# Top-2 gate dispatch: the first group's loads and stores cut at other rows

## The chip, the cores and the metric

The kernel runs on one core of a Trainium2 chip. The metric is the device time of one execution in microseconds. Before the change it is 239.73 us, the median of three runs (239.54 to 239.82). The profile shows the engines that take part: VectorE (DVE) for the products, ScalarE (ACT) for the sigmoids and a few small things, SyncE (SP) as the issuer of most DMAs, and the core's 16 DMA engines, which carry everything between HBM and the on-chip memory.

## The reference

16 x 1024 tokens have 512 numbers each and 8 router logits. For each token the two largest softmax probabilities are normalized to a sum of 1, and the token's numbers are written out twice, once times each of the two weights, the smaller first.

```python
def reference(x, router_logits, k):          # x [16, 1024, 512], logits [16, 1024, 8], k = 2
    logits_max = np.max(router_logits, axis=-1, keepdims=True)
    probs = np.exp(router_logits - logits_max)
    probs = probs / np.sum(probs, axis=-1, keepdims=True)
    topk_indices = np.argsort(probs, axis=-1)[..., -k:]
    topk_probs = np.take_along_axis(probs, topk_indices, axis=-1)
    topk_probs = topk_probs / np.sum(topk_probs, axis=-1, keepdims=True)
    x_expanded = x[:, :, np.newaxis, :].repeat(k, axis=2)
    return (x_expanded * topk_probs[..., np.newaxis]).astype(np.float32)
```

Input and output together are 101.2 MB: 33.6 MB of x, 0.5 MB of logits, and 67.1 MB of output.

## The kernel before, in words

**Rows.** The 16,384 tokens are spread over 128 partitions. A "row" below is one token in each partition, so 128 tokens, and there are 128 rows: 65 in group 0 and 63 in group 1 (`GROUPS`). A row is 2,048 B for each partition in x and 4,096 B in the output, where each token stands twice. In HBM the rows that one partition loads or stores in one DMA lie next to each other, so such a DMA of n rows is 128 runs, one for each partition, eight for each of the 16 DMA engines.

**Buffers.** `xs` holds 65 rows of x. `osp` holds 18 output rows; at the start it also lends its place to the logits and the scratch of the top-2 search. `WA` holds the two weights of every row. Output is built either in `osp` or in `xs` itself, over rows whose x has been used up (a "store in xs" of 16 rows takes the place of 32 rows of x). `STORES` lists for each group, store by store: first row, number of rows, buffer, and place in it.

**Loads.** `LOADS` gives the DMAs of x by rows, group 0 as 6, 28 and 31, group 1 as 4, 28 and 31. `BASE` is the first row of `xs` for each group. All are issued by SyncE (line 139), except the 4-row load of group 1, which ScalarE issues behind a small copy that waits until the last store but one of group 0 has landed (lines 123 to 138). The logits are loaded behind the first 6 rows (lines 144 and 145).

**Weights.** `top2_weights` finds for all rows at once the largest and the second largest logit, by a tournament of maxima and minima, and takes two sigmoids of their difference on ScalarE (lines 37 and 38).

**Products and stores.** For each entry of `STORES`, VectorE multiplies the rows, repeated twice, by their weights (line 164), and the store is issued when the product is done (line 176), by SyncE, except the first store of group 0, which ScalarE issues. A store into place 0 of `osp`, other than the first one, has its product cut in two (lines 151 and 152): the first `FREE[g]` rows go to the front of `osp`, which the store ahead in `osp` hasn't used, and the rest waits for that store to land. In group 1 the last `ACT_ROWS` rows of the first product are computed by ScalarE (lines 155 to 162).

**Order.** DMAs of one queue go in the order of their issue. SyncE's queue (q1 in the profile) has, in this order: the 6 rows, the logits, the other two loads of group 0, its four big stores, two loads of group 1, and its four stores. ScalarE's queue (q10) has the first store of group 0 and the 4-row load of group 1. Loads and stores are kept in the written order (`keep_in_program_order`). The products' order on VectorE isn't written out: it is left to the scheduler, which put them, before the change, in the order of `STORES`, with the cut piece of 3 rows in group 0 behind the product in `xs` and ahead of the remaining 12 rows. A load into rows of `xs` from which a store is still reading waits on SyncE for that store to land.

Of the kernel before, what the change touches and what calls it, by code (L numbers as in the profile page):

```python
# [1 line left out]

# [4 lines left out]

F32 = mybir.dt.float32
ALU = mybir.AluOpType
ACTF = mybir.ActivationFunctionType  # L10
P = 128


def top2_weights(nc, WA, dlt, room, logits, E):

    tt = nc.vector.tensor_tensor
    hi, lo, n = None, None, E  # L20
    while n > 1:
        n //= 2
        if hi is None:
            a, b = logits[:, :, 0:n], logits[:, :, n : 2 * n]
            nhi, nlo = room(n), b
            tt(nhi, a, b, op=ALU.max)  # L26
            tt(nlo, a, b, op=ALU.min)  # L27
        else:
            a, b = hi[:, :, 0:n], hi[:, :, n : 2 * n]
            nhi, nlo, tmp = room(n), room(n), room(n)  # L30
            tt(tmp, lo[:, :, 0:n], lo[:, :, n : 2 * n], op=ALU.max)  # L31
            tt(nlo, a, b, op=ALU.min)  # L32
            tt(nlo, nlo, tmp, op=ALU.max)  # L33
            tt(nhi, a, b, op=ALU.max)  # L34
        hi, lo = nhi, nlo
    tt(dlt, hi[:, :, 0], lo[:, :, 0], op=ALU.subtract)  # L36
    nc.scalar.activation(WA[:, :, 0], dlt, ACTF.Sigmoid, scale=-1.0)  # L37
    nc.scalar.activation(WA[:, :, 1], dlt, ACTF.Sigmoid, scale=1.0)  # L38

GROUPS = [65, 63]

LOADS = [[6, 28, 31], [4, 28, 31]]
BASE = [0, 1]

STORES = [
    [(0, 3, "osp", 0), (3, 15, "osp", 3), (18, 16, "xs", 0), (34, 15, "osp", 0), (49, 16, "xs", 33)],
    [(0, 16, "osp", 2), (16, 16, "xs", 0), (32, 15, "osp", 0), (47, 16, "xs", 32)],
]  # L50

L = 18

FREE = [3, 2]

ACT_ROWS = 2


@with_exitstack
def kernel(  # L60
    ctx: ExitStack,
    tc: tile.TileContext,
    x: bass.AP,
    router_logits: bass.AP,
    k: bass.AP,
    out: bass.AP,
):
    nc = tc.nc
    B, S, D = x.shape
    E = router_logits.shape[-1]  # L70
    N = B * S
    assert int(k) == 2 and E == 8 and N == P * sum(GROUPS)
    M = N // P

    x_v, o_v, rl_v = [], [], []
    t0 = 0
    for n in GROUPS:
        t1 = t0 + P * n
        x_v.append(
            x.rearrange("b s d -> (b s) d")[t0:t1].rearrange("(p m) d -> p m d", p=P)  # L80
        )
        o_v.append(
            out.rearrange("b s k d -> (b s) k d")[t0:t1].rearrange(
                "(p m) k d -> p m k d", p=P
            )
        )
        rl_v.append(
            router_logits.rearrange("b s e -> (b s) e")[t0:t1].rearrange(
                "(p m) e -> p m e", p=P
            )  # L90
        )
        t0 = t1

    wpool = ctx.enter_context(tc.tile_pool(name="wpool", bufs=1))
    xs = wpool.tile([P, max(GROUPS), D], F32)
    osp = wpool.tile([P, L, 2, D], F32)
    WA = wpool.tile([P, M, 2], F32)
    dlt = wpool.tile([P, M], F32)


    flat = osp.rearrange("p l k d -> p (l k d)")
    taken = [0]

    def room(n):
        o = taken[0]
        taken[0] += M * n
        return flat[:, o : o + M * n].rearrange("p (m n) -> p m n", n=n)

    logits = room(E)

    def place(where, at, n):

        if where == "osp":
            return osp[:, at : at + n]
        return xs[:, at : at + 2 * n, :].rearrange("p (r k) d -> p r k d", k=2)

    m0 = 0
    stores = []
    for g, G in enumerate(GROUPS):
        x0, r = BASE[g], 0  # L120
        for n in LOADS[g]:

            late = g == 1 and r == 0
            if late:


                rows = xs[:, x0 : x0 + 2, :]
                pause = nc.scalar.activation(rows, rows, ACTF.Copy)  # L128
                tc.add_manual_dep(
                    pause.ins,  # L130
                    stores[-2].ins.name,
                    mybir.DependencyInfo(
                        mybir.DependencyClass.Sync, mybir.DependencyReason.DATA
                    ),
                    reason="begin when the store ahead of the last has landed",
                )
                tc.keep_in_program_order(pause)
            queue = nc.scalar if late else nc.sync
            load = queue.dma_start(xs[:, x0 + r : x0 + r + n, :], x_v[g][:, r : r + n, :])  # L139
            tc.keep_in_program_order(load)  # L140
            r += n
            if g == 0 and r == 6:
                n0 = GROUPS[0]
                tc.keep_in_program_order(nc.sync.dma_start(logits[:, :n0], rl_v[0]))  # L144
                tc.keep_in_program_order(nc.sync.dma_start(logits[:, n0:], rl_v[1]))  # L145
                top2_weights(nc, WA, dlt, room, logits, E)
        assert r == G
        for r, n, where, at in STORES[g]:
            og = place(where, at, n)

            again = where == "osp" and at == 0 and r > 0
            cuts = [0, FREE[g], n] if again else [0, n]
            if g == 1 and r == 0:
                cuts = [0, n - ACT_ROWS]
                for j in range(n - ACT_ROWS, n):
                    for k2 in range(2):
                        nc.scalar.activation(  # L157
                            og[:, j, k2, :],
                            xs[:, x0 + r + j, :],
                            ACTF.Copy,  # L160
                            scale=WA[:, m0 + r + j, k2 : k2 + 1],
                        )
            for a, b in zip(cuts, cuts[1:]):
                nc.vector.tensor_tensor(  # L164
                    og[:, a:b],
                    xs[:, x0 + r + a : x0 + r + b, :]
                    .unsqueeze(2)
                    .to_broadcast([P, b - a, 2, D]),
                    WA[:, m0 + r + a : m0 + r + b, :]
                    .unsqueeze(3)  # L170
                    .to_broadcast([P, b - a, 2, D]),
                    op=ALU.mult,
                )

            queue = nc.scalar if g == r == 0 else nc.sync
            stores.append(queue.dma_start(o_v[g][:, r : r + n], og))  # L176
            tc.keep_in_program_order(stores[-1])
        m0 += G


# [1 line left out]
_INS = ['x', 'router_logits', 'k']  # L182
_OUTS = [((16, 1024, 2, 512), 'float32')]

_NUMBERS = {'k': 2}


# [26 lines left out]
```

## Time and profile before

| | |
|---|---|
| median of three runs | 239.73 us (239.54 to 239.82) |
| profiled execution, its own time | 239.64 us |
| span of the profiled execution, first to last instruction | 237.9 us |
| DMA packets, bytes, mean rate | 2448, 101.19 MB, 425 GB/s |
| HBM read and written | 34.08 MB and 67.11 MB |

The page of the profile gives each engine's busy time, the DMA queues, the chain of work that ended last, and groups of instructions by line with their mean time. `L164 DVE TENSOR_TENSOR osp<-xs,WA 128x15360` is the product of line 164 on VectorE from `xs` and `WA` into `osp` with 15,360 elements for each partition, that is 15 output rows of 1,024. `SPq` and `ACTq` are the issuing of DMAs by SyncE and ScalarE: the time beside it is the issue alone, not the transfer. In brackets stands how long the engine was idle before an instruction, and what ended that. A row of the view by stretches has start and end, length, busy time and number of instructions of VectorE, ScalarE and GpSimd, the granted clock of TensorE (unused here), the mean busy share of the 16 DMA engines and the GB/s that they moved. There, packets are counted whole in the stretch in which they start, so that short stretches show shares above 1 and below. A row of the DMA view has queue, packets, MB, and share of the 16 engines in the stretch asked for.

### The profile page before, as it was taken

How to read it: one execution, taken by the hardware profiler on the slowest of the kernel's cores; microseconds unless marked ns; L12 is line 12 of the kernel's file. 1: busy time of each engine (PE TensorE's matmuls, PEld its weight loads, DVE VectorE, ACT ScalarE, POOL GpSimd, SP SyncE). 2: the span in 40 equal slices, each digit the busy share in tenths (PEclk: the TensorE clock that was granted, in tenths of full speed). 3: DMA queues.
4: the chain of work that ended last, by engine and by line, in shares of the span. 5: the costliest groups of instructions: out<-in, count | busy, mean ns of one | idle time of the engine just before them, and what ended most of it. 6: DMA issues, size and time to landing. Idle time of an engine off the chain costs nothing.

```text
span 237.9 us, 111 instructions
## 1 busy us (share of the span) xinstructions
DVE 139.8 (59%) x22; ACT 5.4 (2%) x8; POOL 0.2 (0%) x4
## 2 busy tenths in 40 slices
DVE  0650499999689999200000009999976999950000
ACT  2000000000000000010000003000000000000000
POOL 0000000000000000000000000000000000000000
DMA  7989998989998989989998999898998989989894
GB/s 266 550 357 481 441 408 375 486 351 496 397 463 353 529 362 465 496 353 415 555 397 350 444 479 470 384 507 364 485 397 386 496 353 507 465 362 518 353 529 176
DMA packets 2448, 101.19 MB, mean 425 GB/s; under 512 B 272, under 2 KB 400, under 8 KB 528
## 3 DMA queue, kind: packets, MB, share of 16 engines
q1 hardware_dynamic: 2160, 98.57, 96.2%
q10 hardware_dynamic: 288, 2.62, 2.6%
HBM read 34.08 MB, written 67.11 MB: 425 GB/s over the span
## 4 chain that ended last, share of the span: by engine, by line
DMA 49%; DVE 39%; SPq 1%; issue 0%; DVEq 0%
DMA xs<-in_x_dram 29%; DVE osp L164 25%; DMA out_dram<-osp 19%; DVE xs L164 14%; SPq L144 0%; SPq L145 0%; SPq L139 0%; SPq L176 0%; DVEq L164 0%
## 5 line engine op out<-in xcount | busy, mean ns | idle before, releaser
L164 DVE TENSOR_TENSOR osp<-xs,WA 128x3072 f32<-128x3072 f32 (+5 forms) x7 | 67.2, 9604 | 63.5 <-DMA xs<-in_x_dram 56.9
L164 DVE TENSOR_TENSOR xs<-xs,WA 128x16384 f32<-128x16384 f32 x4 | 68.9, 17225 | 0.2
L26 DVE TENSOR_TENSOR osp<-osp 128x512 f32<-128x512 f32 x1 | 0.7, 691 | 8.1 <-DMA osp<-in_router_logits_dram 8.1
L157 ACT ACTIVATE osp<-xs,WA 128x512 f32<-128x512 f32 x4 | 2.6, 709 | 37.6 <-DMA xs<-in_x_dram 37.6
L128 ACT ACTIVATE xs<-xs 128x1024 f32<-128x1024 f32 x1 | 1.1, 1056 | 91.1 <-DMA out_dram<-osp 91.1
L37 ACT ACT_TABLE_LOAD x1 | 1.3, 1283 | 0.7 <-PEq L195 0.7
L27 DVE TENSOR_TENSOR osp<-osp 128x512 f32<-128x512 f32 x1 | 0.7, 691 | 0.0
L32 DVE TENSOR_TENSOR osp<-osp 128x256 f32<-128x256 f32 (+1 forms) x2 | 0.7, 352 | 0.0
L34 DVE TENSOR_TENSOR osp<-osp 128x256 f32<-128x256 f32 (+1 forms) x2 | 0.7, 351 | 0.0
L33 DVE TENSOR_TENSOR osp<-osp 128x256 f32<-128x256 f32 (+1 forms) x2 | 0.7, 351 | 0.0
L31 DVE TENSOR_TENSOR osp<-osp 128x256 f32<-128x256 f32 (+1 forms) x2 | 0.7, 350 | 0.0
L37 ACT ACTIVATE WA<-dlt 128x128 f32<-128x128 f32 x1 | 0.3, 315 | 10.0 <-DVE dlt L36 10.0
L36 DVE TENSOR_TENSOR dlt<-osp 128x128 f32<-128x128 f32 x1 | 0.3, 291 | 0.0
L38 ACT ACTIVATE WA<-dlt 128x128 f32<-128x128 f32 x1 | 0.3, 298 | 0.0
L195 POOL MEMSET const-uint8-127<- 128x1 uint8 x1 | 0.1, 102 | 0.0
L195 POOL MEMSET const-bfloat16-1.0<- 128x1 bf16 x1 | 0.1, 101 | 0.0
L195 POOL MEMSET const-float32-0.0<- 128x1 f32 x1 | 0.1, 98 | 0.2 <-issue 0.2
L195 POOL MEMSET const-float32-1.0<- 128x1 f32 x1 | 0.1, 98 | 0.0
## 6 DMA issues: line engine op xcount, KB each, us to landing
out_dram<-osp SPq DMA_DIRECT2D x3, 7680.0 KB, 23.3
xs<-in_x_dram SPq DMA_DIRECT2D x2, 7936.0 KB, 40.7
xs<-in_x_dram SPq DMA_DIRECT2D x2, 7168.0 KB, 35.1
xs<-in_x_dram SPq DMA_DIRECT2D x1, 1536.0 KB, 5.9
out_dram<-osp ACTq DMA_DIRECT2D x1, 1536.0 KB, 24.8
xs<-in_x_dram ACTq DMA_DIRECT2D x1, 1024.0 KB, 24.8
osp<-in_router_logits_dram SPq DMA_DIRECT2D x1, 260.0 KB, 6.2
osp<-in_router_logits_dram SPq DMA_DIRECT2D x1, 252.0 KB, 6.3
```

Source lines behind the costliest of these rows:

```text
L26: tt(nhi, a, b, op=ALU.max)
L27: tt(nlo, a, b, op=ALU.min)
L31: tt(tmp, lo[:, :, 0:n], lo[:, :, n : 2 * n], op=ALU.max)
L32: tt(nlo, a, b, op=ALU.min)
L33: tt(nlo, nlo, tmp, op=ALU.max)
L34: tt(nhi, a, b, op=ALU.max)
L36: tt(dlt, hi[:, :, 0], lo[:, :, 0], op=ALU.subtract)
L37: nc.scalar.activation(WA[:, :, 0], dlt, ACTF.Sigmoid, scale=-1.0)
L128: pause = nc.scalar.activation(rows, rows, ACTF.Copy)
L157: nc.scalar.activation(og[:, j, k2, :], xs[:, x0 + r + j, :], ACTF.Copy, scale=WA[:, m0 + r + j, k2 : k2 + 1],)
L164: nc.vector.tensor_tensor(og[:, a:b], xs[:, x0 + r + a : x0 + r + b, :] .unsqueeze(2) .to_broadcast([P, b - a, 2, D]), WA[:, m0 + r + a : ...
L195: nc = _bacc.Bacc("TRN2", target_bir_lowering=False, num_devices=1)
```

## The change

Three lists of numbers change, all for group 0; nothing else does.

```diff
-LOADS = [[6, 28, 31], [4, 28, 31]]
+LOADS = [[6, 30, 29], [4, 28, 31]]
 BASE = [0, 1]
 
 STORES = [
-    [(0, 3, "osp", 0), (3, 15, "osp", 3), (18, 16, "xs", 0), (34, 15, "osp", 0), (49, 16, "xs", 33)],
+    [(0, 1, "osp", 0), (1, 16, "osp", 2), (17, 16, "xs", 0), (33, 16, "osp", 0), (49, 16, "xs", 33)],
     [(0, 16, "osp", 2), (16, 16, "xs", 0), (32, 15, "osp", 0), (47, 16, "xs", 32)],
 ]
 
 L = 18
 
-FREE = [3, 2]
+FREE = [2, 2]
```

- The second load of group 0 takes rows 6 to 35, not 6 to 33, and the third has the remaining 29.
- The first store, ScalarE's, has 1 row, not 3. The four big ones have 16 rows each; before, they had 15, 16, 15 and 16. The last one is as before.
- The first product that is cut, that of the third big store, is cut after 2 rows, not after 3, and these 2 rows (33 and 34) are now in the second load; the 3 before (34 to 36) were in the third.
- The compiled program has as many instructions on each engine as before. VectorE's order in group 0 differs in one point: the cut piece now stands ahead of the product in `xs`, and behind it before.

```
before: 128x3072 (osp), 128x15360 (osp), 128x16384 (xs), 128x3072 (osp), 128x12288 (osp), 128x16384 (xs)
after:  128x1024 (osp), 128x16384 (osp), 128x2048 (osp), 128x16384 (xs), 128x14336 (osp), 128x16384 (xs)
```

## The prediction

> **What bounds the kernel now.** I read the page first, for the shares of engines and queues.
>
> ```profile
> span 237.9 us, 111 instructions
> DVE 139.8 (59%) x22; ACT 5.4 (2%) x8; POOL 0.2 (0%) x4
> q1 hardware_dynamic: 2160, 98.57, 96.2%
> q10 hardware_dynamic: 288, 2.62, 2.6%
> ```
>
> The two DMA queues (q1 is filled by SyncE, q10 by ScalarE) kept the 16 DMA engines at 96.2% + 2.6% = 98.8% of the span. VectorE works 59% of it. Next come the busy times by stretch, in which a packet counts where it starts; the columns behind the times are VectorE, ScalarE, GpSimd, clock, DMA share, GB/s.
>
> ```profile
> 0.00:1.70 1.70, 0.00 (x0) 0.97 (x1) 0.20 (x4) 1.00 0.00 0
> 1.70:1.80 0.10, 0.00 (x0) 0.10 (x1) 0.00 (x0) 1.00 2.93 737
> 2.00:236.60 234.60, 139.79 (x22) 4.14 (x8) 0.00 (x0) 1.00 1.00 431
> 236.60:237.90 1.30, 0.00 (x0) 0.00 (x0) 0.00 (x0) 1.00 0.00 0
> 13.54:15.65 2.11, 2.11 (x1) 0.00 (x0) 0.00 (x0) 1.00 1.00 435
> 23.03:25.56 2.53, 0.00 (x0) 0.00 (x0) 0.00 (x0) 1.00 1.01 368
> 42.35:44.69 2.34, 2.31 (x2) 0.00 (x0) 0.00 (x0) 1.00 1.00 434
> 44.69:47.14 2.45, 2.45 (x1) 0.00 (x0) 0.00 (x0) 1.00 1.02 415
> 47.14:47.65 0.51, 0.51 (x1) 0.00 (x0) 0.00 (x0) 1.00 4.46 1928
> ```
>
> From 2.00 to 236.60 us the share is 1.00: the DMA engines never stop. Both kernels move the same bytes, so the change can win next to nothing in the middle; it can lose, wherever it lets the engines run dry, and such a hole goes into the time one to one. So the question is what happens at the two places where a store must be ready before the work ahead of it in the queue is gone. The rows from 42.35 to 44.69 are one round: each engine takes one partition's run of the second load, 31 rows x 2,048 B = 63,488 B, in 2.34 us. That is 434 GB/s, or 27.1 GB/s for one engine; I price all moved bytes by it. The row at 47.14 holds the start of the first big store: the last load packets, begun at 44.69, end at 47.14 on the first engine and 47.65 on the last, and the store's follow with no hole.
>
> The timeline of the first group tells when the stores were issued (start, length, engine, line), and the chain of waits when the second load and the first big store landed:
>
> ```profile
> 12.52 3.36 DVE L164 TENSOR_TENSOR osp<-xs,WA 128x3072 f32<-128x3072 f32 x1 [0.58 <-ACT WA L38]
> 15.91 0.38 ACTq L176 DMA_DIRECT2D out_dram<-osp  x1
> 26.82 16.16 DVE L164 TENSOR_TENSOR osp<-xs,WA 128x15360 f32<-128x15360 f32 x1 [10.94 <-DMA xs<-in_x_dram]
> 43.00 0.35 SPq L176 DMA_DIRECT2D out_dram<-osp  x1
> 43.01 17.22 DVE L164 TENSOR_TENSOR xs<-xs,WA 128x16384 f32<-128x16384 f32 x1
> 60.15 3.35 DVE L164 TENSOR_TENSOR osp<-xs,WA 128x3072 f32<-128x3072 f32 x1
> 60.26 0.34 SPq L176 DMA_DIRECT2D out_dram<-xs  x1
> 66.15 12.96 DVE L164 TENSOR_TENSOR osp<-xs,WA 128x12288 f32<-128x12288 f32 x1 [2.64 <-DMA out_dram<-osp]
> 79.13 0.33 SPq L176 DMA_DIRECT2D out_dram<-osp  x1
> ```
>
> ```profile
> 26.79 0.02 issue
> ...
> 43.00 23.12 DMA out_dram<-osp
> ```
>
> The first big store is issued at 43.00, 4.14 us before the loads ahead of it end. The second, at 60.26, has the first one's eight packets ahead of it (15 rows x 4,096 B = 61,440 B, 2.27 us each, so until 47.14 + 8 x 2.27 = 65.28): 5.0 us.
>
> How much of such a margin an issue needs is shown by the very first load of the program:
>
> ```profile
> 0.73 0.37 SPq L139 DMA_DIRECT2D xs<-in_x_dram  x1
> xs<-in_x_dram SPq DMA_DIRECT2D x1, 1536.0 KB, 5.9
> ```
>
> Issued at 0.73, its first packet starts between 1.70 and 1.80 (the windows above): 1.0 us, on idle engines. So the two margins are really about 3.1 and 4.0 us. Its landing, 5.9 us after the issue (second row, from the page's DMA issues), bounds what idle engines lose beside this: less 1.0 of way, 3.6 for the bytes, and the 0.84 that the first big store's landing lay behind its last packet (43.00 + 23.12 = 66.12 against 65.28), 0.4 us are left.
>
> **The change part by part.** *The first store is 1 row, not 3.* VectorE's first product has 1,024 elements for each partition, not 3,072. A row costs 1.07 us (the next fence: 2.29 for 2,048 against 3.36 for 3,072), so it takes 3.36 - 2.14 = 1.22, and ScalarE issues at 15.91 - 2.14 = 13.77. Its packets shrink from 12,288 to 4,096 B, 0.453 to 0.151 us. With eight for each engine, the DMA work up to the end of the loads shrinks by 8 x 0.302 = 2.42 us. The bytes aren't saved: the next big store has them.
>
> ```profile
> 157.53 17.23 DVE L164 TENSOR_TENSOR xs<-xs,WA 128x16384 f32<-128x16384 f32 x1
> 174.67 2.29 DVE L164 TENSOR_TENSOR osp<-xs,WA 128x2048 f32<-128x2048 f32 x1
> ```
>
> *The loads are 6, 30 and 29.* The first big product needs the 30. Eight packets get 2 rows longer each: 8 x 4,096 B / 27.1 GB/s = 1.21 us. In between come the small store's turns. The DMA view of 15 to 26 us has
>
> ```profile
> q1 hardware_dynamic: 64, 3.67, 82.2%
> q10 hardware_dynamic: 48, 0.59, 12.5%
> ```
>
> that is, 48 / 16 = 3 turns of the small store for each engine before the load landed at 26.79. Issued 2.14 us earlier, about one load packet, it gets a fourth. Landing: 26.79 + 1.21 + 4 x 0.151 - 3 x 0.453 = 27.25 us. The uncertain part is the round from 23.03 to 25.56, which took 2.53 us where the same bytes took 2.11 in the round at 13.54; if that doesn't recur, the load lands at 26.8.
>
> A rule of the Trainium skill says otherwise about turns: DMA: Bandwidth & Descriptors, "Queues, rings and completion order", has an engine drain a packet of typically 9 to 17 descriptors from one queue before it goes to the next, and "The descriptor swizzle" there counts 9 for each engine in a transfer to 128 partitions, which would send a small store in one turn. By it all eight packets would go ahead of the load's end and the sum below would be 4 x 0.151 = 0.6 us more, an estimate; the three turns above and the rounds below contradict it (one run of one partition at a time), so I keep the row.
>
> *The first big store is 16 rows, not 15.* The product has 16,384 elements, 17.22 us as at 43.01. It ends at 27.25 + 0.03 + 17.22 = 44.50, and the store is issued there, 1.5 us later than before. Nothing waits behind it on SyncE but the later stores. The loads meanwhile end 2.42 us earlier: 47.14 - 2.42 = 44.72 on the first engine, 45.23 on the last. The store so comes while the last load packets run, but with only 0.22 us left, and it needs 1.0. Its first packet starts at 45.51 and the engines stand idle for **0.79 us**. Bounds: if the long round doesn't recur, the issue falls at 44.1 and the hole is 0.4; if the idle engines start as slowly as the first load did, 0.4 more, 1.2. I take the way alone, since that load reads HBM and the store doesn't.
>
> *The split piece moves.* FREE is 2, so the first piece of the third big store is rows 33 and 34, which are in the 30-row load, and not rows 34 to 36, which were in the last. Compiled, VectorE's order becomes 16,384 into osp, the 2,048 piece, 16,384 into xs, where the piece stood behind xs before. So the second big store is held up by the piece. Before, it was issued 60.26 - 43.00 = 17.26 us after the first; now it is 17.26 + 2.29 - 0.08 (products overlap that much, 60.15 against 43.01 + 17.22) = 19.47. The first big store now takes 8 x 65,536 B / 27.1 GB/s = 19.35. As the first store starts as late as its issue allows, the second comes 19.47 - 19.35 = **0.12 us** late as well. Bounds: 0, if a slow start stretches the store ahead, and 0.5, if the 0.4 of a slow start falls on this one.
>
> *The rest of the group.* The third store's remaining 14 rows still wait for the first big store's landing, as the 12 did at 66.15; it comes at 45.51 + 19.35 + 0.84 = 65.70. They take as long as this product of group two:
>
> ```profile
> 142.35 15.09 DVE L164 TENSOR_TENSOR osp<-xs,WA 128x14336 f32<-128x14336 f32 x1 [45.98 <-DMA xs<-in_x_dram]
> ```
>
> So the issue is at 80.8. The store ahead ends at 45.51 + 0.12 + 2 x 19.35 = 84.33, so 3.5 us are left of which 1.0 is needed. Covered; were that cover gone, the price would be what is missing of it. Before the fourth big store both kernels have stored 49 rows, so group two gets its rows, loads and margins moved by the holes alone and is worth nothing.
>
> Sum: 0.79 + 0.12 = 0.91, on the profiled execution's 239.64 us (span 237.9, 1.74 around it): **240.5 us**; the median of the runs shown is 239.73, so 0.8 us or 0.33% above.
>
> **The rivals.** *The store still arrives in time (no change).* Then the change does what its few words say. It needs 0.8 us, say by no long round (0.4) and a shorter way from issue to packet. For it: VectorE's issue at 44.1 is possible. Against: the loads' end would move up with the long round too. 239.6 to 240.0, taken as 239.8.
>
> *A store needs far longer on loaded engines.* ScalarE's issue at 15.91 shows its first packet 4.05 us later, as the DMA views of 15.9 to 19.95 (q1 alone) and 28 to 40 (turns one by one) have it:
>
> ```profile
> q1 hardware_dynamic: 19, 1.09, 65.8%
> ...
> q1 hardware_dynamic: 64, 4.06, 78.1%
> q10 hardware_dynamic: 64, 0.79, 15.3%
> ```
>
> I read that as up to two load packets that had been taken already. Against a long way speaks group two, where a store issued at 157.51 on SyncE's queue follows the loads at 160.08 with no hole:
>
> ```profile
> 157.51 0.34 SPq L176 DMA_DIRECT2D out_dram<-osp  x1
> 157.00:160.08 3.08, 2.99 (x2) 0.00 (x0) 0.00 (x0) 1.00 0.76 330
> 160.08:160.60 0.52, 0.52 (x1) 0.00 (x0) 0.00 (x0) 1.00 4.67 2017
> ```
>
> So the way takes at most 160.08 - 157.51 = 2.57. At that limit the hole is 44.50 + 2.57 - 44.72 = 2.35, with the second store's 0.12 that is 239.64 + 2.47 = 242.1. The Trainium skill, DMA: Bandwidth & Descriptors, "Latency and other measured facts", has HBM latency at 0.2 us on average and 2 us at high load, which leans this way; no row here splits the latency from the queue.
>
> *Faster.* One mechanism: reads beside the small store ran long, 0.42 us in the round at 23.03 and 0.11 in that at 44.69 (2.45 against 2.34). If turns of 0.151 us leave them their full rate, the group is 0.53 us shorter: 239.1. It decides only if the store arrives at the loads' end, then 44.72 - 0.53 = 44.19, so is issued by 43.2 and the 30 rows have landed by 25.9. Against: that is 0.9 us before the 28 rows landed.
>
> **How the numbers follow.** My forecast (holes of 0.4 to 1.6 us, 240.0 to 241.2) gets 0.58, in time 0.22, the long way 0.14, faster 0.06. About 0.2%, 0.5 us, is what a measurement can tell here, so slower starts at 240.2: 0.55 of the forecast and all of the long way, 0.69; within, 0.03 and the case in time, 0.25; faster 0.06. The range goes from 239.7, half of the case in time, to 242.1.
>
> **What would show it.** The 30-row load landing near 27.2 and the first big store issued near 44.5; a DMA share of 0 for some 0.8 us before its first packets at 45.5; a second issue some 19.5 us behind the first, with a share just below 1 between the two stores; no hole ahead of the third. Wrong it is if the store's packets follow the loads' without a hole, or start over 2 us after its issue, or if a hole stands elsewhere.

## The result, and the profile after

The changed kernel takes 241.17 us (median of six runs, 240.96 to 241.44) against 239.68 for the kernel before on the same chips; the ratio is 1.0056 with a 95% interval of 1.0039 to 1.0073. It is slower, as forecast, and inside the range, but the loss is 1.5 us where 0.91 were worked out. Of the 83 runs of the kernel before that stand beside the changed kernel and the experiments below, nine took 240.6 to 241.6 us; no trace of such a run was kept. The page of the profiled execution (241.31 us around its span):

```profile
span 239.5 us, 113 instructions
DVE 139.7 (58%) x22; ACT 5.4 (2%) x8; POOL 0.2 (0%) x4
q1 hardware_dynamic: 2160, 99.62, 96.8%
q10 hardware_dynamic: 288, 1.57, 1.6%
```

VectorE's work is the same. The queues' packets took 98.4% of a longer span: 235.7 us, 0.6 more than before (98.8% of 237.9 is 235.0) for the same bytes, and the rest of the loss is idle time. The view by stretches shows the predicted hole (busy times, clock, DMA share, GB/s at the end):

```profile
23.40:25.90 2.50, 0.00 (x0) 0.00 (x0) 0.00 (x0) 1.00 0.98 419
42.00:44.20 2.20, 2.20 (x1) 0.00 (x0) 0.00 (x0) 1.00 1.00 432
44.20:45.32 1.12, 1.12 (x2) 0.00 (x0) 0.00 (x0) 1.00 0.01 0
45.32:45.47 0.15, 0.15 (x1) 0.00 (x0) 0.00 (x0) 1.00 16.37 6991
62.29:64.72 2.43, 1.50 (x1) 0.00 (x0) 0.00 (x0) 1.00 1.00 432
64.72:65.00 0.28, 0.00 (x0) 0.00 (x0) 0.00 (x0) 1.00 8.67 3745
```

The last load packets start at 42.00 and take 2.20 us, so the first engine is done at 44.20. For 1.12 us no data packet starts; then those of the first big store start on all 16 engines within 0.15 us. In the kernel before that took 0.51 us (47.14 to 47.65), so the hole put the engines in step. There is no such row ahead of the second big store: the round that starts at 62.29 ends at 64.72, and the next begins there.

The timeline has the issues:

```profile
14.14 0.38 ACTq L176 DMA_DIRECT2D out_dram<-osp  x1
27.22 19.43 DVE L164 TENSOR_TENSOR osp<-xs,WA 128x16384 f32<-128x16384 f32 x2 [13.11 <-DMA xs<-in_x_dram]
44.48 0.35 SPq L176 DMA_DIRECT2D out_dram<-osp  x1
46.57 17.22 DVE L164 TENSOR_TENSOR xs<-xs,WA 128x16384 f32<-128x16384 f32 x1
63.81 0.34 SPq L176 DMA_DIRECT2D out_dram<-xs  x1
80.45 0.33 SPq L176 DMA_DIRECT2D out_dram<-osp  x1
104.11 1.06 ACT L128 ACTIVATE xs<-xs 128x1024 f32<-128x1024 f32 x1 [91.26 <-DMA out_dram<-osp]
143.72 2.56 ACT L157 ACTIVATE osp<-xs,WA 128x512 f32<-128x512 f32 x4 [38.55 <-DMA xs<-in_x_dram]
181.98 14.03 DVE L164 TENSOR_TENSOR osp<-xs,WA 128x13312 f32<-128x13312 f32 x1 [3.55 <-DMA out_dram<-osp]
```

The last three rows are good marks, since each waits for a landing on the slowest engine: ScalarE's copy for the third big store of group 0, its first product in group 1 for the 28 rows, and VectorE's later product for the first store of group 1. The same marks before:

```profile
103.62 1.06 ACT L128 ACTIVATE xs<-xs 128x1024 f32<-128x1024 f32 x1 [91.13 <-DMA out_dram<-osp]
...
142.25 2.56 ACT L157 ACTIVATE osp<-xs,WA 128x512 f32<-128x512 f32 x4 [37.57 <-DMA xs<-in_x_dram]
...
180.33 14.03 DVE L164 TENSOR_TENSOR osp<-xs,WA 128x13312 f32<-128x13312 f32 x1 [3.37 <-DMA out_dram<-osp]
```

So the changed kernel is late by 0.49 us at 104.11, by 1.47 at 143.72 and by 1.65 at 181.98, and keeps that to the end (span 239.5 against 237.9). The hole and all else in group 0 come to 0.49 us net. Two thirds of the loss, 0.98 + 0.18, arise in a part of the program that wasn't changed. The view by stretches shows it in rounds of 16 packets, one for each engine: of 65,536 B in the last store of group 0, and of 63,488 B (the last row of each fence) where the loads of group 1 end and its first store follows. First the changed kernel, then the kernel before:

```profile
105.92:108.34 2.42, 0.00 (x0) 0.00 (x0) 0.00 (x0) 1.00 1.01 433
108.35:111.04 2.69, 0.00 (x0) 0.00 (x0) 0.00 (x0) 1.00 1.00 390
119.51:121.93 2.42, 0.00 (x0) 0.00 (x0) 0.00 (x0) 1.00 1.00 433
122.23:124.92 2.69, 0.00 (x0) 0.00 (x0) 0.00 (x0) 1.00 1.07 390
159.19:161.89 2.70, 2.70 (x1) 0.00 (x0) 0.00 (x0) 1.00 0.99 376
```

```profile
107.52:109.93 2.41, 0.00 (x0) 0.00 (x0) 0.00 (x0) 1.00 1.00 435
121.12:123.53 2.41, 0.00 (x0) 0.00 (x0) 0.00 (x0) 1.00 1.03 445
157.74:160.08 2.34, 2.34 (x1) 0.00 (x0) 0.00 (x0) 1.00 1.00 434
```

In the changed kernel the store rounds at 108.35 and at 122.23 move the same bytes in 2.69 us and more (a DMA share of 1.07 means that the packets of the second outlast the stretch: 2.9 us each on average). Both are rounds of writes with reads right behind them: the first turn of ScalarE's 4-row load, and the 28 rows. Before, such rounds take 2.41. Reads behind a round are not enough, though: the rounds between the two, such as that at 119.51, have further turns of the 4-row load behind them and take 2.42. The third long round, at 159.19, is one of reads with writes behind it, 2.7 us in place of 2.34; it lies between the last two marks. By shares times lengths, the three rounds are 1.1 us longer than those before.

### The profile page after: what moved, and what is told of

Same layout as the page of the kernel before. It is cut to its first block, busy times and chain, and to the rows that moved or that the text cites. A ratio compares the mean times of both kernels' runs of the same rounds, so it can differ in the third digit from the quotient of the medians.

```text
span 239.5 us, 113 instructions
## 1 busy us (share of the span) xinstructions
DVE 139.7 (58%) x22; ACT 5.4 (2%) x8; POOL 0.2 (0%) x4
## 4 chain that ended last, share of the span: by engine, by line
DMA 48%; DVE 40%; SPq 1%; issue 0%; DVEq 0%
DMA xs<-in_x_dram 29%; DVE osp L164 26%; DMA out_dram<-osp 18%; DVE xs L164 14%; SPq L144 0%; SPq L145 0%; SPq L139 0%; SPq L176 0%; DVEq L164 0%
## 5 line engine op out<-in xcount | busy, mean ns | idle before, releaser
L164 DVE TENSOR_TENSOR osp<-xs,WA 128x2048 f32<-128x2048 f32 (+4 forms) x7 | 67.1, 9604 | 64.9 <-DMA xs<-in_x_dram 59.2
```

Source lines behind the costliest of these rows:

```text
L164: nc.vector.tensor_tensor(og[:, a:b], xs[:, x0 + r + a : x0 + r + b, :] .unsqueeze(2) .to_broadcast([P, b - a, 2, D]), WA[:, m0 + r + a : ...
```

## The experiments

All were measured in rounds beside the kernel before, whose median was 239.64 to 239.66 us in each group. The first four ask whether the loss hangs on the hole.

**Loads alone.** The stores, cuts and order of before:

```diff
-LOADS = [[6, 28, 31], [4, 28, 31]]
+LOADS = [[6, 30, 29], [4, 28, 31]]
```

> The kernel before with the loads 6, 30 and 29 alone; stores and cut as before. The 30 rows land near 28.0 us (2 rows more, the same small store), the first big store is issued near 44.2, some 3 us ahead of the end of the loads (47.1). Theory A (the loss comes from the hole ahead of the first big store, and from long rounds that the hole brings on later): no hole, no loss, 239.7. Theory B (part of the loss comes with the new cut of the stores, hole or not): 239.7 too. Were the loads a cost of their own, 240 or more.

Ratio 1.0018 (0.9999 to 1.0036), median 240.40, with single runs from 239.66 to 241.27. The first big store was issued at 44.23, the copy behind the third store began at 103.44 (before: 103.62), so the loads cost group 0 nothing. In the profiled run the first store of group 1 was noticed at 180.85, 0.52 later than before: one engine lagged. Both theories had 239.7, and both missed: by the medians this kernel is 0.7 us slower, though the interval still holds 1. The run with ScalarE's help, below, shows such a lag more plainly.

**Stores alone.** The changed kernel with the old loads:

```diff
-LOADS = [[6, 30, 29], [4, 28, 31]]
+LOADS = [[6, 28, 31], [4, 28, 31]]
```

> The changed kernel with the loads of before, 6, 28 and 31. The 28 rows land near 26.0, the first big store is issued near 43.3, its packets can start 0.9 later, near 44.2, which is where the loads end. The cut piece then needs the last load and stands behind the product in xs again. Theory A: hardly a hole (under 0.2 us), no long rounds later, 239.6 to 239.9. Theory B: the stores' cut is that of the changed kernel, so the part of the loss beyond the hole stays, 240.2 to 240.5.

Ratio 1.0000 (0.9984 to 1.0017), median 239.94. The timeline and the stretches of this kernel:

```profile
43.03 0.35 SPq L176 DMA_DIRECT2D out_dram<-osp  x1
```

```profile
44.05:44.75 0.70, 0.70 (x1) 0.00 (x0) 0.00 (x0) 1.00 3.47 1498
```

Its 16 first packets start between 44.05 and 44.75, over the same 0.7 us in which the loads' last ones end, at least 1.0 us behind the issue; no hole. With two rows less in the load the hole is closed, and 1.2 us of the loss of 1.5 are gone by the medians; 0.28 us are left, and 0.4 is the interval's upper end. But the trace has more to say. Two of the marks, and the three rounds that ran long in the changed kernel:

```profile
103.02 1.06 ACT L128 ACTIVATE xs<-xs 128x1024 f32<-128x1024 f32 x1 [90.38 <-DMA out_dram<-osp]
142.26 2.56 ACT L157 ACTIVATE osp<-xs,WA 128x512 f32<-128x512 f32 x4 [38.19 <-DMA xs<-in_x_dram]
```

```profile
106.94:107.39 0.45, 0.00 (x0) 0.00 (x0) 0.00 (x0) 1.00 5.67 2330
120.79:123.49 2.70, 0.00 (x0) 0.00 (x0) 0.00 (x0) 1.00 1.07 388
157.75:160.41 2.66, 2.66 (x1) 0.00 (x0) 0.00 (x0) 1.00 0.96 382
```

At the copy this kernel is 0.60 us ahead of the kernel before, since its loads end 3.1 us sooner on the first engine (44.05 against 47.14) where 2.42 were reckoned. At the 28 rows it is 0.01 behind: the 0.60 is lost again, with no hole ahead (in the changed kernel the same stretch lost 0.98). The three rounds run long here too: all 16 packets of the first start within the 0.45 us of its row and take 5.67 x 0.45 = 2.55 us on average, those of the second 2.9, and the reads of the third 2.55 in place of 2.34. So the equal time is a gain and a loss that cancel. Theory A is right that the hole's price goes with the hole, and wrong that there are no long rounds without one; theory B has the long rounds right and the time, 240.2 to 240.5, too long. Nor must the engines be in step for such a round: ahead of the first one they stood up to 0.45 us apart, close to the 0.5 of the kernel before.

**ScalarE takes 2 rows of the first big product.** The changed kernel otherwise:

```diff
-            if g == 1 and r == 0:
+            if (g, r) in ((1, 0), (0, 1)):
                 cuts = [0, n - ACT_ROWS]
```

> The changed kernel, with the last 2 rows of the first big product done by ScalarE, so that the store is issued near 42.3 in place of 44.5, well ahead of the end of the loads (44.2). Loads, stores, cut and order stay as changed. Theory A: no hole and no long rounds, 239.4 to 239.8, all of the loss is gone. Theory B: only the hole goes, 240.2 to 240.5.

Ratio 1.0054 (1.0038 to 1.0069), median 241.23: a miss for both. The store was issued at 42.09 and its packets follow the loads' with no hole:

```profile
41.90:44.10 2.20, 2.20 (x2) 0.00 (x0) 0.00 (x0) 1.00 1.00 432
44.10:44.80 0.70, 0.70 (x2) 0.00 (x0) 0.00 (x0) 1.00 3.47 1498
```

The copy behind the third store begins at 102.91, 0.7 us ahead of before: without the hole group 0 gains. But the 28 rows are noticed at 143.25. The last round of group 0's last store ran long, again with no hole ahead:

```profile
120.51:123.24 2.73, 0.00 (x0) 0.00 (x0) 0.00 (x0) 1.00 1.00 387
```

The end of its trace, in the DMA view of 233.0 to 234.1 and of 235.5 to 235.6, shows one thing more:

```profile
q1 hardware_dynamic: 16, 1.05, 219.8%
...
q1 hardware_dynamic: 1, 0.07, 151.1%
```

All engines start a packet within the first stretch; 15 are done with it and the kernel by 236.5 (234.1 + 2.42), but one has yet another to go, at 235.5, and ends at 237.9: that engine is at least 1.4 us behind, and the kernel ends with it. So the loss behind group 0 has a second form, one engine that lags, and neither form needs a hole.

**A hole in the kernel before.** VectorE made late by computing rows 3 to 6 twice:

```diff
+            if g == 0 and r == 3:
+                nc.vector.tensor_tensor(og[:, 0:4], xs[...], WA[...], op=ALU.mult)
```

> The kernel before, with the first 4 rows of the first big product computed twice, so that VectorE is 4.3 us later and the first big store is issued near 47.3. Its packets start near 48.2, and the loads end at 47.1 to 47.6: a hole of 0.5 to 1.0 us, with the old loads and the old cut. Theory A: the engines leave the hole closer in step (starts 0.15 us apart, not 0.5), long rounds follow between 105 and 160 us, 241.0 to 241.4. Theory B: the hole alone, 240.4 to 240.6.

Ratio 1.0084 (1.0061 to 1.0107), median 242.02, 2.4 us above before. The timeline, and the stretches:

```profile
47.54 0.35 SPq L187 DMA_DIRECT2D out_dram<-osp  x1
```

```profile
47.06:48.38 1.32, 1.28 (x2) 0.00 (x0) 0.00 (x0) 1.00 0.01 0
48.38:48.54 0.16, 0.16 (x1) 0.00 (x0) 0.00 (x0) 1.00 14.40 6144
108.98:111.68 2.70, 0.00 (x0) 0.00 (x0) 0.00 (x0) 1.00 1.00 388
122.87:125.56 2.69, 0.00 (x0) 0.00 (x0) 0.00 (x0) 1.00 1.08 390
```

The issue was a little later than reckoned, and the hole 1.32 us, so the time lies above theory A's figures too. The engines start in step again, within 0.16 us, and the same two rounds of the last store run long again. So with the old loads and the old cut, which show no long rounds there by themselves, a hole brings them, and the loss is 1.0 us more than the hole. A hole is thus one way to the long rounds; the new cut alone was another.

**Is it the mixing of two queues?** Four kernels with the 4-row load of group 1 on SyncE's queue, behind the last store, and without ScalarE's copy:

```diff
-            late = g == 1 and r == 0
+            late = False
```

> The kernel before, with the 4-row load of group 1 issued by SyncE behind the last store of group 0, ahead of the 28 rows, and without ScalarE's copy ahead of it. The same bytes, but no packets of two queues mixed after 41 us. Theory C (the second part of the loss arises where ScalarE's 4-row load shares the engines with the last store and with the next load, from 104 us to 161 us, by long rounds or by one engine that falls behind, and the kernel before mostly escapes it): as before, 239.3 to 239.8. Theory A (long rounds follow the hole wherever it is, at each switch of stores and loads): 239.6 too. If keeping the loads behind the store costs something of its own, above 240.

> The changed kernel with the same edit. The hole ahead of the first big store stays (first packets 0.9 us behind its issue, engines idle for some 0.95 us). Theory C: the hole alone is left, 240.2 to 240.6, no long rounds from 104 to 161 us, the engines land the last store within 0.5 us of each other. Theory A: hole and long rounds, 241.0 to 241.4.

> The changed kernel with 2 rows of the first big product on ScalarE (no hole, yet 241.2 with the mixed queues, where one engine fell 1.9 us behind), and with the 4-row load on SyncE. Theory C: no hole and no mixed stretch, 239.0 to 239.6, no engine behind. If the late loss is not the mixing's, 240.5 to 241.4 again.

> The kernel before with 4 rows of the first big product computed twice (a hole of 1.2 us, 242.0 with the mixed queues), and with the 4-row load on SyncE. Theory C: the hole alone, 240.7 to 241.1. Theory A: 241.8 to 242.1 as with the mixed queues.

In this order: 239.71 us, ratio 0.9993 (0.9976 to 1.0009); 241.20, 1.0055 (1.0036 to 1.0073); 240.91, 1.0038 (1.0019 to 1.0056); 242.08, 1.0096 (1.0072 to 1.0121). Theory C falls: with one queue alone the changed kernel loses as much, and the kernel with ScalarE's help, for which it had 239.0 to 239.6, still takes 240.91. Its stretches, then those of the kernel before with the same edit:

```profile
44.10:45.15 1.05, 1.05 (x2) 0.00 (x0) 0.00 (x0) 1.00 0.01 0
117.88:120.30 2.42, 0.00 (x0) 0.00 (x0) 0.00 (x0) 1.00 1.00 433
120.30:122.99 2.69, 0.00 (x0) 0.00 (x0) 0.00 (x0) 1.00 1.18 390
```

```profile
117.21:119.62 2.41, 0.00 (x0) 0.00 (x0) 0.00 (x0) 1.00 1.00 435
119.62:122.03 2.41, 0.00 (x0) 0.00 (x0) 0.00 (x0) 1.00 1.00 435
```

Only the last round of the store runs long now, the one with loads right behind it, and by more (a share of 1.18 over 2.69 us: some 3.2 us for each packet on average). So the mixing isn't needed; the long round of the store stands at its switch from writes to reads.

**VectorE's order undone.** The changed kernel with its products kept in the written order:

```diff
-                nc.vector.tensor_tensor(
+                product = nc.vector.tensor_tensor(
...
+                tc.keep_in_program_order(product)
```

> The changed kernel with VectorE's products kept in the written order, so that the 2-row piece stands behind the product in xs again and the second big store is issued 2.2 us earlier (near 61.6, not 63.8). The prediction had 0.12 us for this move; the trace of the changed kernel shows no hole ahead of the second big store. Theory D (the move costs nothing): 241.0 to 241.3, as the changed kernel. The prediction's term: 0.1 less, which a median hardly shows, but a hole between the two stores in the changed kernel that goes here would.

240.96 us (240.95 to 241.13), ratio 1.0060 (1.0046 to 1.0074). The second store was issued at 61.41 in place of 63.81, and the loss stayed; the median is just below theory D's range. The move of the piece costs nothing that shows, but a median can't tell 0.1 us.

**A hole in group 1.** The first try computed rows 0 to 2 of its first product twice:

> The kernel before, with 3 rows of the first product of group 1 computed twice: its first store is issued near 160.8 in place of 157.5, and the engines, which end the loads at 160.1 to 160.6, stand idle until 161.7, for 1.1 to 1.6 us. Theory E (the second loss arises at switches between stores and loads, and depends on how the 16 engines stand to each other there; a hole behind the last load, with stores alone to follow, brings none): the hole alone, 240.8 to 241.2, no long rounds behind it. Rival (a hole brings some 1 us of long rounds wherever it is): 241.8 to 242.3.

239.58 us, ratio 1.0000 (0.9991 to 1.0010), because the edit did nothing: these rows come with the 4-row load, and VectorE computed them at 129.68, in idle time. The second try took rows 4 to 6, which come with the 28 rows:

```diff
+            if g == 1 and r == 0:
+                nc.vector.tensor_tensor(og[:, 4:7], xs[...], WA[...], op=ALU.mult)
```

> The kernel before, with rows 4 to 6 of the first product of group 1 computed twice; these rows come with the 28-row load, so this time VectorE really is 3.3 us later: first store of group 1 issued near 160.8, its packets from 161.7, the loads end at 160.1 to 160.6, a hole of 1.1 to 1.6 us with stores alone to follow. Theory E (a hole costs itself; long rounds come only at a later switch from stores to loads): 240.8 to 241.3, no long rounds behind the hole. Rival (a hole brings some 1 us of long rounds wherever it is): 241.8 to 242.3.

241.34 us (241.28 to 241.56), ratio 1.0072 (1.0058 to 1.0086), 1.68 us above before. Its timeline and stretches:

```profile
161.02 0.34 SPq L183 DMA_DIRECT2D out_dram<-osp  x1
```

```profile
160.12:161.85 1.73, 1.64 (x2) 0.00 (x0) 0.00 (x0) 1.00 0.00 0
161.85:162.02 0.17, 0.17 (x1) 0.00 (x0) 0.00 (x0) 1.00 14.45 6168
166.73:238.50 71.77, 44.99 (x4) 0.00 (x0) 0.00 (x0) 1.00 1.00 431
```

A hole of 1.73 us on the first engine costs 1.68, and from 166.73 on the engines, in step as after every hole, run at their full 431 GB/s. No reads follow here. The time is just above theory E's range, as the hole was longer than reckoned, and below its rival's: this hole is paid once, with no switch between reads and writes behind it. What came on top in the other kernels arose at such switches.

**Pulling the engines apart again.** The changed kernel with three idle loads behind the first big store:

```diff
+            if g == 0 and r == 1:
+                for p0, k in ((0, 12), (32, 8), (64, 4)):
+                    nc.sync.dma_start(spare[p0 : p0 + k], x_v[0][:k, 0:2]...)
```

> The changed kernel with three idle loads of 4 KB runs into a spare tile, for 12, 8 and 4 partitions, issued behind the first big store: they hold up some of the engines by 0.15, 0.3 and 0.46 us against the others, so that the engines, in step behind the hole (landing within 0.2 us), stand some 0.5 us apart again, as in the kernel before. Theory E: the late long rounds (1.1 us at 108, 122 and 150 to 160 us) shrink to 0.3 or less, 240.3 to 240.8 with the 0.46 that the idle loads cost. Rival (the standing of the engines has no part in it): 241.5 to 241.8.

242.04 us (241.84 to 242.21), ratio 1.0102 (1.0088 to 1.0116): above both. The idle loads cost far more than 0.46: they are reads, and the store round ahead of them ran long where the one before it took 2.42, so they brought a switch of their own, as the stretches show:

```profile
59.99:62.41 2.42, 2.42 (x1) 0.00 (x0) 0.00 (x0) 1.00 1.00 433
62.41:65.05 2.64, 1.49 (x1) 0.00 (x0) 0.00 (x0) 1.00 1.08 422
```

The copy behind the third store began at 105.41, 1.30 later than in the changed kernel. From there to the 28 rows the marks lost nothing more (144.13 - 105.41 = 38.72, against 38.63 before and 39.61 in the changed kernel), but a mark shows the slowest engines alone. The last round of the store, in the DMA view of 122.56 to 122.76, has 12 engines ahead of the other four:

```profile
q1 hardware_dynamic: 12, 0.79, 1118.5%
```

Their packets take 11.185 x 0.20 x 16 / 12 = 3.0 us on average. So the engines were apart and the round ran long all the same; theory E had these rounds shrink to 0.3 us in all. What part the standing of the engines has stays open.

## Why the prediction was right, and where it was short

- *The 30 rows' landing*: 27.25 predicted; VectorE starts at 27.22. That it fits so well is in part luck. The long round did not recur (419 GB/s at 23.40, against 368 at 23.03 before), which by the prediction's own words gives 26.8; but the engines stood further apart, their packets of the load's last round starting over 0.72 us (23.57 to 24.29) against 0.46 before, and VectorE waits for the last of them. Were the small store sent in one turn, as the Trainium skill has it in DMA: Bandwidth & Descriptors, "Queues, rings and completion order", the landing would have been 0.6 later by that working; it wasn't, and the DMA view of 15 to 25 us has 48 of its packets, three single turns for each engine.
- *The issue of the first big store*: 44.50 predicted, 44.48 measured.
- *The way to its first packet*: 1.0 predicted, 45.32 - 44.48 = 0.84 measured. The other two holes give the same: 48.38 - 47.54 = 0.84 in the kernel before made late, and 161.85 - 161.02 = 0.83 in group 1, where the prediction's rival had allowed up to 2.57.
- *The end of the loads*: 44.72 predicted, 44.20 measured, since the reads kept their full rate. So the hole came to 1.12 us on the first engine, inside its bounds of 0.4 to 1.2. The faster rival's mechanism was thus real, and gave its half microsecond; it made the hole longer instead of the kernel shorter.
- *The second big store*: 0.12 us predicted for the moved piece, none found. It was issued 63.81 - 44.48 = 19.33 behind the first, not 19.47, and its packets follow on the round's end.
- *The third big store*: 80.8 predicted, 80.45 measured, no hole ahead of it.
- *The step that failed*: "group two gets its rows, loads and margins moved by the holes alone and is worth nothing". Group 0 lost 0.49 net, less than the 0.91 of the sum: the 0.12 didn't come, and of the hole's 1.12 the loads' earlier end gives back 0.52. And 0.98 + 0.18 were added between the third store's landing and group 1's first store's. The sign was right and the hole was there; the size was short by a term that the prediction didn't have. That 241.17 still lies in the band forecast for the holes alone, 240.0 to 241.2, is luck; with group 0's 0.49 alone it would have been 240.2.

What the runs show of that term: its place is the last store of group 0 and the loads behind it, up to the first store of group 1. In the changed kernel it is three rounds at switches between writes and reads, 2.7 to 2.9 us in place of 2.4 or 2.3. It doesn't need the new loads (stores alone has the rounds), the new cut (the kernel before with a hole has them), ScalarE's queue, or VectorE's new order; nor does it need the hole, since stores alone and ScalarE's help have long rounds without one. (Each kernel has a single trace behind this.) The kernel before shows none there in its trace, nor does it with the 4-row load on SyncE. With ScalarE's help one engine fell behind as well, and with the new loads alone that was all that showed.

So the loss of the changed kernel is made of three parts. The loads end sooner than reckoned, which by itself is worth 0.60 at the copy, as stores alone shows. The hole takes that and more: at the copy the changed kernel is 104.11 - 103.02 = 1.09 behind stores alone, close to the hole's 1.12. Then the marks lose 1.16 more up to the first store of group 1, and the long rounds, 1.1 us on average over the engines, stand in that stretch. Why a switch runs long in some of these kernels and not in others is open.

No version tried beats the kernel before: stores alone and the 4-row load on SyncE's queue can't be told from it, 1.0000 and 0.9993, with 1 inside both intervals (by the medians stores alone is 0.28 us slower).

## What to carry to other kernels

Where the DMA engines never stop, ask of every edit how far ahead of the queue's end each store is issued, and count the way from issue to first packet (0.84 us here) against that margin: moving work out of the queue's head and onto the engine that feeds it shrinks the margin from both ends (here 4.14 - 0.84 = 3.3 us were there; 2.9 went to the sooner end of the loads and 1.5 to the later product, which leaves a hole of 1.1). A hole was paid at its full length. Time made up by faster reads is worth nothing where what follows isn't ready. And an equal time is not an equal course: stores alone gained 0.6 us in one stretch and lost it in the next, which only the marks along the trace show.

## What the runs showed of the hardware that was not expected

- The same 16 packets of 65,536 B took 2.41 to 2.42 us in one kernel and 2.69 or more in another at the same place, with the same bytes before and behind: writes with reads behind them, in kernels with a hole ahead and without. A round of reads with writes behind it did the same (2.7 against 2.34).
- In one program a single DMA engine fell at least 1.4 us behind the other 15 and kept that lag to the end, so that one engine's packet decided the time.
- Idle engines all started within 0.15 to 0.17 us, 0.83 to 0.84 us behind the issue, in each of three holes (1.12 to 1.73 us).
